# A decoder layer on one core: twelve small loads between weight chunks, three groups of transposes moved, and a projection that takes its chunks in pairs

## The chip, the core and the metric

The kernel runs on one core of a Trainium2 chip. A core has a matrix engine (TensorE, PE in the profile; its weight loads have a row of their own, PEld), three engines for elementwise work (VectorE = DVE, ScalarE = ACT, GpSimd = POOL) and SyncE (SP), which here only issues transfers. Each engine works through its own list of instructions in order and waits on semaphores for the others. Transfers between main memory (HBM) and the on-chip memory (SBUF) are issued by SP or POOL and carried out by 16 DMA engines. [...]

The metric is the device time of one execution in microseconds (us). The kernel before took 1500.24 us (median of three runs: 1500.24, 1496.19, 1501.05).

## The reference

One layer of a decoder with 256 positions and a width of 2048, in float32. What matters here:

```python
def reference(x, ...):                       # x: (1, 256, 2048)
    h = rms_norm(x, norm_mix_pre)
    y = hybrid_mixer(h, w_in, ...)           # two attention branches, gated, summed, @ w_out
    x = x + rms_norm(y, norm_mix_post)       # the second use of x; the scale norm_mix_post
    h = rms_norm(x, norm_ffn_pre)
    y = conv_ffn(h, w_up, conv_w, conv_b, w_down)
    return x + rms_norm(y, norm_ffn_post)

def hybrid_mixer(h, ...):
    c_q, c_kv, k_r, q_s, k_s, v_s, gates = split(h @ w_in)
    q  = rms_norm(c_q, g_q) @ w_q_up         # latent attention: c_q (512 wide), c_kv (256 wide)
    kv = rms_norm(c_kv, g_kv) @ w_kv_up
    ...                                      # o_a: dense causal, o_b: sliding window
    g = sigmoid(gates)
    merged = g[0] * (o_a @ w_o_mla) + g[1] * (o_b @ w_o_swa)
    return merged @ w_out

def conv_ffn(h, w_up, ...):                  # w_up: 2048 x 11264 (two halves of 5632)
    a, b = split(h @ w_up)
    c = conv_b + conv_w[0]*a[t-2] + conv_w[1]*a[t-1] + conv_w[2]*a[t]
    return (gelu(c) * b) @ w_down
```

## The kernel before, in words

**Products in three parts.** A float32 operand is split into a coarse part (`hi`) and the remainder (`lo`), both in a format that TensorE takes at full rate. A product is hi*hi + hi*lo + lo*hi, the sum of three matmuls.

**Weights come as chunks.** Every weight is read once from HBM. `wchunk` (L106) fetches 128 x 1024 numbers (512 KB) into one of three `raw` buffers by a transfer that SP issues; ACT casts it to `whi` (L124), DVE subtracts to `wlo` (L125). There are five `whi` and five `wlo` buffers, so the two engines can be some five chunks ahead of TensorE. A `raw` buffer is free for the next transfer when both casts of its chunk are done, a `whi` or `wlo` buffer when TensorE's last matmul on it is done.

**Two forms of product.** `gemm` (L153) holds the activations as TensorE's weights and streams 512 columns of the weight matrix: twelve matmuls of 512 columns per chunk (L149 to L151), into two accumulators of 128 rows each. `gemm_t` (L181), used for the up projection `w_up` alone, holds the weight matrix as TensorE's weights and streams the activations. The hi and lo parts of the 256 positions lie side by side, so that the hi part of a weight block meets both in one matmul of 512 columns (L189) and the lo part meets the hi half alone in a matmul of 256 columns (L193). One chunk is eight matmuls of 512 columns and then eight of 256, over four accumulators. The up projection has eleven blocks of 512 columns for each half (a and b); the first block of half a goes through `gemm`, which leaves 21 calls of `gemm_t` of eight chunks each, 168 chunks.

**Deferred work.** `at(t, f)` puts f on a list under step t, and `tick()`, called once per chunk after the chunk's matmuls, runs what stands under the current step. So a group of transposes that is put at `now[0] + 1` gets its place on TensorE behind the second chunk of the product that follows. The Tile scheduler may still move an instruction in an engine's list, except where `keep_in_program_order` or a manual schedule forbids it; the lists it made are shown below.

**The places that the change touches.**

- The latents c_q and c_kv: `latent` (L487) scales them and gives `tr` (L501), which transposes a pair of 128-column blocks on TensorE into one PSUM tile (`cqT`, `ckT`), each half followed by a cast on ACT and a subtraction on DVE (L224, L225). `k_rope` (L536) does the same for the rope key.
- The merge of the branches, once for each block of 512 columns: `gemm` with `wo_a` (w_o_mla, 8 chunks), then two DVE instructions per half of the rows (L772, L773) form `lta` = gate * product + the other branch, and `m_cols` (L749) transposes `lta` on TensorE in two groups of four (`mT`, L754), which become the operand of the product with `w_out`.
- `x2` and `gpost`: the second copy of x (eight tiles of 256 KB) and the scale of the norm after the mixer, spread to all 128 partitions (1 MB). POOL issues them (L744, L779) before and beside the first `wo_a` product. `gpost` is first read when the first `w_out` block is done (L791), `x2` when the last one is (`resid`, L800).
- The up projection: behind each half a, ACT and DVE run the convolution and the gelu (`conv_next`, L891, with `conv_a`), four pieces of 256 columns, under the steps of half b's first chunks; behind half b, `conv_b` (L896).

Of the kernel before, what the change touches and what calls it, by code (L numbers as in the profile page):

```python
# [19 lines left out]
P = 128  # L20
D = 2048
S = 256
NT = 2
# [18 lines left out]
def trunk_layer(ctx, tc, x, g_mix_pre, g_mix_post, g_ffn_pre, g_ffn_post, w_in, g_q, w_q, g_kv, w_kv,  # L42
                sinks, rel, wo_a, wo_b, w_out, w_up, conv_w, conv_b, w_down, rope_tab, strip_sel, out):
    nc = tc.nc
# [14 lines left out]
    def sb(pl, shape, name, dt=F32, tag=None, bufs=None):  # L59
        return pl.tile(shape, dt, name=name, tag=tag or name, **({"bufs": bufs} if bufs else {}))  # L60
# [45 lines left out]
    def wchunk(src, shape, own=None, rawp=None):  # L106
        i = cnt[0]
        cnt[0] += 1
        n = int(np.prod(shape))
        raw = rawp.tile([P, 1024], F32, name=f"raw{i}", tag="xraw") if rawp else \  # L110
            ring.tile([P, 1024], F32, name=f"raw{i}", tag="raw", bufs=RAW)
        dst = raw[:, :n]
        if len(shape) == 2:
            dst = dst.rearrange("p (a b) -> p a b", a=shape[0])
        elif len(shape) == 3:
            dst = dst.rearrange("p (a b c) -> p a b c", a=shape[0], b=shape[1])
        if len(shape) == 3:
            for k in range(shape[0]):
                nc.sync.dma_start(dst[:, k], src[:, k])
        else:  # L120
            nc.sync.dma_start(dst, src)
        hi, lo = ((own or ring).tile([P, 1024], F32R, name=f"w{part}{i}", tag="w" + part)
                  for part in ("hi", "lo"))
        act.copy(hi[:, :n], raw[:, :n])  # L124
        vec.tensor_tensor(lo[:, :n], raw[:, :n], hi[:, :n].bitcast(F32), op=ALU.subtract)  # L125
        return hi, lo
# [5 lines left out]
    def at(t, *fs):  # L132
        steps[max(t, now[0])].extend(fs)

    def tick():
        for f in steps.pop(now[0], ()):
            f()
        now[0] += 1

    def drain():  # L140
        while steps:
            tick()
# [37 lines left out]

    def gemm_t(xs, w, nk, c0, acc):  # L181

        for k in range(0, nk, 2):
            src = w[k * P:(k + 2) * P, c0:c0 + 512].rearrange("(a p) n -> p a n", p=P)
            hi, lo = wchunk(src, [2, 512])
            for j in range(2):
                for i in range(4):
                    c = j * 512 + i * P
                    pe.matmul(acc[i], hi[:, c:c + P], xs(k + j), start=k + j == 0, stop=False)  # L189
            for j in range(2):  # L190
                for i in range(4):
                    c = j * 512 + i * P
                    pe.matmul(acc[i][:, 0:256], lo[:, c:c + P], xs(k + j)[:, 0:256], start=False, stop=k + j == nk - 1)  # L193
            tick()

    def rsqrt(v, n, name, pl):
        y = sb(pl, [P, n], f"{name}_y")
# [323 lines left out]
    acc, _ = gemm(XH, XL, w_in, 0, KT, 0, 512)  # L521
    nrm, tr = latent(acc, QR, 32, cqh, cql, "cq")
    nrm()
    at(now[0] + 3, lambda tr=tr: tr(0))
    at(now[0] + 4, lambda tr=tr: tr(1))
    acc, _ = gemm(XH, XL, w_in, 0, KT, C_KV, KVR + ROPE)
    krd = []
    for t in range(NT):
# [12 lines left out]

    nrm, tr = latent(acc, KVR, 36, [ckh], [ckl], "ck")
    nrm()
    at(now[0] + 2, k_rope)
    at(now[0] + 3, lambda tr=tr: tr(0))


    ta_d = dram.tile([4, NT, P, 512], F32, name="ta_d")
# [190 lines left out]
    MH_, ML_ = pair_view(mth), pair_view(mtl)  # L739
    sb(p3, [P, 16], "pad_c")  # L740
    x2 = [[sb(p3, [P, 512], f"x2_{t}_{j}") for j in range(4)] for t in range(NT)]
    for t in range(NT):
        for j in range(4):
            pool.dma_start(x2[t][j], x[t * P:(t + 1) * P, j * 512:(j + 1) * 512])  # L744
    es6, p6 = open_pool("p6")
    esx, px = open_pool("px", bufs=EXTRA)
    es4, p4 = open_pool("p4")
# [1 line left out]
    def m_cols(p, ld):  # L749
        pt = pst.tile([P, 512], F32, name=f"mT{p}", tag="t")  # L750
        for i in range(2):
            for t in range(NT):
                c = (2 * (p % 2) + i) * P
                pe.transpose(pt[:, i * 256 + t * P:i * 256 + (t + 1) * P], ld[t][0][:, c:c + P], ident)  # L754
        split_to(mth[p][:, :], mtl[p][:, :], pt, 0.5)

    def merge_loads(j):
# [6 lines left out]
            ld.append((a, b))  # L764
        return ld

    for j in range(4):
        ld = merge_loads(j)
        acc, _ = gemm(AH, AL, wo_a, 0, KT, 512 * j, 512)
        for t in range(NT):  # L770
            a, b = ld[t]
            vec.scalar_tensor_tensor(a, a, 1.0, acc[t], op0=ALU.add, op1=ALU.mult)  # L772
            vec.tensor_tensor(a, a, b, op=ALU.add)  # L773
        for p in range(2):
            at(now[0] + 1 + p, lambda p=2 * j + p, ld=ld: m_cols(p, ld))


    gpost = sb(p6, [P, D], "gpost", tag="gp")
    pool.dma_start(gpost, g_mix_post.partition_broadcast(P))  # L779
    yg = [[sb(p6, [P, 512], f"yg_{t}_{j}", tag="f" + "ab"[t], bufs=4) for j in range(4)] for t in range(NT)]  # L780
    blocks = [(0, 512), (512, 512), (1024, 512), (1536, 256), (1792, 256)]
    NB = len(blocks)
# [56 lines left out]
    for b in range(4):  # L839
        c0, n = W_BLOCKS[b]  # L840
        last = b == 3
        acc, todo = gemm(MH_, ML_, w_out, 0, KT, c0, n, split=last, extra={i: (px,) for i in range(EXTRA)} if last else None)
        if b == 0:
            drain()
            es4.close()
            es8, p8 = open_pool("p8")
        if last:
            y_evac(acc, b, 0)
            resid(0)
            for f in todo:  # L850
                f()
            y_evac(acc, b, 1)
        else:
            for t in range(NT):
                y_evac(acc, b, t)
# [193 lines left out]
```

## Time and profile before

| what | value |
|---|---|
| median of three runs | 1500.24 us (1496.19 to 1501.05) |
| the profiled execution's own time | 1497.73 us |
| its span in the trace | 1495.9 us |
| granted TensorE clock, mean | 0.997 of full speed |
| TensorE busy | 1477.5 us (99%), 7853 matmuls |
| DVE, ACT busy | 988.6 us (66%), 802.2 us (54%) |
| moved by DMA | 285.52 MB, 191 GB/s on the mean |
| w_out, w_o_mla, w_up chunks, issue to landing (median) | 4.1, 4.5, 4.5 us |

How to read it: the page gives busy time for each engine and the chain of work that ended last. "L124" is a line of the kernel, and a group is named by what it writes and reads (`mT<-ident,lta`). A matmul's duration in a row (some 390 ns for 512 columns) holds its way through the array and overlaps the next one, so the rate is read from the distance of two starts. "[2.31 <-DVE lta L773]" behind a row means that the engine sat idle for 2.31 us before it, ended by that instruction. Times in rows are from the start of the span.

### The profile page before, as it was taken

How to read it: one execution, taken by the hardware profiler on the slowest of the kernel's cores; microseconds unless marked ns; L12 is line 12 of the kernel's file. 1: busy time of each engine (PE TensorE's matmuls, PEld its weight loads, DVE VectorE, ACT ScalarE, POOL GpSimd, SP SyncE). 2: the span in 40 equal slices, each digit the busy share in tenths (PEclk: the TensorE clock that was granted, in tenths of full speed). 3: DMA queues.
4: the chain of work that ended last, by engine and by line, in shares of the span. 5: the costliest groups of instructions: out<-in, count | busy, mean ns of one | idle time of the engine just before them, and what ended most of it. 6: DMA issues, size and time to landing. Idle time of an engine off the chain costs nothing.

```text
span 1495.9 us, 21394 instructions
## 1 busy us (share of the span) xinstructions
PE 1477.5 (99%) x7853; PEld 1265.2 (85%) x7853; DVE 988.6 (66%) x1775; ACT 802.2 (54%) x1332; POOL 66.8 (4%) x114
## 2 busy tenths in 40 slices
PE   8999999999999999999999999999999999999997
PEld 6888888888899987888888888888888888888887
DVE  5688884444766764565677877876444677787555
ACT  6588874434555553444575555564444555565442
POOL 2123210000000002000000000000000000000000
PEclk9999999999999999999999999999999999999999
DMA  7766656666655558766656556566556556655663
GB/s 235 223 177 166 167 169 191 208 210 208 180 158 160 167 160 288 250 208 197 207 170 193 184 178 185 179 193 209 196 190 197 174 176 211 195 184 182 200 197 113
DMA packets 160808, 285.52 MB, mean 191 GB/s; under 512 B 18419, under 2 KB 33893, under 8 KB 160448
## 3 DMA queue, kind: packets, MB, share of 16 engines
q1 hardware_dynamic: 154736, 264.81, 56.2%
q0 software_dynamic: 5968, 19.36, 5.2%
q8 instruction: 61, 1.00, 0.3%
q14 instruction: 43, 0.35, 0.1%
HBM read 277.79 MB, written 6.34 MB: 190 GB/s over the span
## 4 chain that ended last, share of the span: by engine, by line
PE 92%; DVE 3%; DMA 2%; ACT 2%; issue 1%; SPq 0%; DVEq 0%; ACTq 0%
PE accg L150 17%; PE accg L151 17%; PE accg L149 17%; PE accb L189 11%; PE acca L189 10%; PE accb L193 6%; PE acca L193 5%; DMA raw<-in_w_in_dram 1%; DVE wlo L125 1%; DMA raw<-in_w_o_mla_dram 1%; PE mpo L701 1%; PE ms L667 1%; ACT p L427 1%; ACT whi L124 1%; PE qn L630 1%
## 5 line engine op out<-in xcount | busy, mean ns | idle before, releaser
L125 DVE TENSOR_TENSOR wlo<-raw,whi 128x1024 fp32r<-128x1024 f32 (+2 forms) x501 | 608.7, 1216 | 439.0 <-ACT whi L124 436.4
L124 ACT CAST whi<-raw 128x1024 fp32r<-128x1024 f32 (+2 forms) x501 | 522.9, 1045 | 547.9 <-PE accg L151 297.4
L149 PE MATMUL accg<-whi,ah 128*128 128x512 f32 (+2 forms) x896 | 343.8, 384 | 0.4 <-ACT whi L124 0.4
L150 PE MATMUL accg<-wlo,ah 128*128 128x512 f32 (+2 forms) x896 | 341.3, 381 | 0.5 <-DVE wlo L125 0.5
L151 PE MATMUL accg<-whi,al 128*128 128x512 f32 (+2 forms) x896 | 340.8, 380 | 0.0
L151 PEld LDWEIGHTS accg<-whi,al 128*128 128x128 f32 x896 | 168.5, 188 | 31.4
L150 PEld LDWEIGHTS accg<-wlo,ah 128*128 128x128 f32 x896 | 168.6, 188 | 30.8 <-DVE wlo L125 1.6
L149 PEld LDWEIGHTS accg<-whi,ah 128*128 128x128 f32 x896 | 168.5, 188 | 29.9 <-ACT whi L124 1.1
L149 PE MATMUL accg<-whi,bh 128*128 128x512 f32 x272 | 107.3, 394 | 0.0
L150 PE MATMUL accg<-wlo,bh 128*128 128x512 f32 x272 | 106.4, 391 | 0.0
L151 PE MATMUL accg<-whi,bl 128*128 128x512 f32 x272 | 106.3, 391 | 0.0
L189 PE MATMUL accb<-bh,whi 128*128 128x512 f32 x352 | 88.6, 393 | 0.0
L189 PE MATMUL accb<-bl,whi 128*128 128x512 f32 x352 | 88.4, 393 | 0.0
L189 PE MATMUL acca<-bh,whi 128*128 128x512 f32 x320 | 80.3, 392 | 0.0
L189 PE MATMUL acca<-bl,whi 128*128 128x512 f32 x320 | 80.1, 392 | 0.0
L189 PEld LDWEIGHTS accb<-bh,whi 128*128 128x128 f32 x352 | 63.2, 189 | 11.6 <-ACT rfrow L836 0.3
L189 PEld LDWEIGHTS accb<-bl,whi 128*128 128x128 f32 x352 | 63.3, 189 | 11.3
L189 PEld LDWEIGHTS acca<-bh,whi 128*128 128x128 f32 x320 | 57.5, 189 | 10.6 <-DVE ds L953 0.3
L189 PEld LDWEIGHTS acca<-bl,whi 128*128 128x128 f32 x320 | 57.6, 189 | 10.3
L151 PEld LDWEIGHTS accg<-whi,bl 128*128 128x128 f32 x272 | 51.3, 189 | 10.8
L149 PEld LDWEIGHTS accg<-whi,bh 128*128 128x128 f32 x272 | 51.4, 189 | 10.4
L150 PEld LDWEIGHTS accg<-wlo,bh 128*128 128x128 f32 x272 | 51.4, 189 | 10.3
(339 smaller groups left out, 1934.3 us busy)
## 6 DMA issues: line engine op xcount, KB each, us to landing
raw<-in_ffn_w_up_dram SPq DMA_DIRECT2D x176, 512.0 KB, 4.5
raw<-in_w_in_dram SPq DMA_DIRECT2D x111, 512.0 KB, 4.3
raw<-in_ffn_w_down_dram SPq DMA_DIRECT2D x88, 512.0 KB, 4.4
raw<-in_w_o_swa_dram SPq DMA_DIRECT2D x32, 512.0 KB, 4.2
raw<-in_w_o_mla_dram SPq DMA_DIRECT2D x32, 512.0 KB, 4.5
raw<-in_w_out_dram SPq DMA_DIRECT2D x32, 512.0 KB, 4.1
raw<-in_mla_w_q_up_dram SPq DMA_DIRECT2D x48, 128.0 KB, 2.7
bias<-strip POOLq DMA_DIRECT2D x16, 256.0 KB, 4.0
```

The costliest lines, as they stand in the source:

```text
L124: act.copy(hi[:, :n], raw[:, :n])
L125: vec.tensor_tensor(lo[:, :n], raw[:, :n], hi[:, :n].bitcast(F32), op=ALU.subtract)
L149: pe.matmul(o, ah, bh, start=start, stop=False)
L150: pe.matmul(o, ah, bl, start=False, stop=False)
L151: pe.matmul(o, al, bh, start=False, stop=stop)
L189: pe.matmul(acc[i], hi[:, c:c + P], xs(k + j), start=k + j == 0, stop=False)
L193: pe.matmul(acc[i][:, 0:256], lo[:, c:c + P], xs(k + j)[:, 0:256], start=False, stop=k + j == nk - 1)
L427: act.activation(pb[:, i, a:b], pb[:, i, a:b], AF.Exp, bias=st["nm"][:, i, t:t + 1], accum_out=st["sm"][:, i, t:t + 1])
L630: pe.matmul(o, wh, ch(k), start=k == 0, stop=False)
L667: pe.matmul(o, w, v_, start=n == 0, stop=False)
L701: pe.matmul(o, w(t), p_[:, c], start=n == 0, stop=n == 5)
```

## The change

Three edits that do not depend on each other:

1. **Loads.** The eight transfers of `x2` leave POOL and go to SP, one at a time, under the steps 34, 37, ... 55 counted from the start of the `wo_a` product; `gpost` goes from one transfer of 1 MB to four of 256 KB, under the steps 19, 22, 25, 28. `keep_in_program_order` holds them at their places between SP's weight transfers. The `drain()` behind the first `w_out` block is taken out, since it would run the later steps at once.
2. **Transposes.** The groups of c_q go one step later (4 and 5 for 3 and 4), those of the rope key and of c_kv two steps (4 and 5 for 2 and 3), those of the merged rows one step (2 and 3 for 1 and 2).
3. **Pairs.** `gemm_t` fetches two chunks, runs the sixteen matmuls of 512 columns of both, and then the sixteen of 256. The steps tick behind each half of the 512s.

```diff
     def gemm_t(xs, w, nk, c0, acc):
-        for k in range(0, nk, 2):
-            src = w[k * P:(k + 2) * P, c0:c0 + 512].rearrange("(a p) n -> p a n", p=P)
-            hi, lo = wchunk(src, [2, 512])
-            for j in range(2):
-                for i in range(4):
-                    c = j * 512 + i * P
-                    pe.matmul(acc[i], hi[:, c:c + P], xs(k + j), start=k + j == 0, stop=False)
-            for j in range(2):
-                for i in range(4):
-                    c = j * 512 + i * P
-                    pe.matmul(acc[i][:, 0:256], lo[:, c:c + P], xs(k + j)[:, 0:256], start=False, stop=k + j == nk - 1)
-            tick()
+        for k in range(0, nk, 4):
+            ws = []
+            for kk in (k, k + 2):
+                ws.append(wchunk(w[kk * P:(kk + 2) * P, c0:c0 + 512].rearrange("(a p) n -> p a n", p=P), [2, 512]))
+            for n, (hi, _) in enumerate(ws):
+                for j in range(2):
+                    for i in range(4):
+                        c = j * 512 + i * P
+                        pe.matmul(acc[i], hi[:, c:c + P], xs(k + 2 * n + j), start=k + 2 * n + j == 0, stop=False)
+                tick()
+            for n, (_, lo) in enumerate(ws):
+                for j in range(2):
+                    for i in range(4):
+                        c = j * 512 + i * P
+                        pe.matmul(acc[i][:, 0:256], lo[:, c:c + P], xs(k + 2 * n + j)[:, 0:256], start=False,
+                                  stop=k + 2 * n + j == nk - 1)
...
-    at(now[0] + 3, lambda tr=tr: tr(0))
-    at(now[0] + 4, lambda tr=tr: tr(1))
+    at(now[0] + 4, lambda tr=tr: tr(0))
+    at(now[0] + 5, lambda tr=tr: tr(1))
...
-    at(now[0] + 2, k_rope)
-    at(now[0] + 3, lambda tr=tr: tr(0))
+    at(now[0] + 4, k_rope)
+    at(now[0] + 5, lambda tr=tr: tr(0))
...
-    for t in range(NT):
-        for j in range(4):
-            pool.dma_start(x2[t][j], x[t * P:(t + 1) * P, j * 512:(j + 1) * 512])
...
+    gpost = sb(p6, [P, D], "gpost", tag="gp")
+
+    def load_gpost(j):
+        c = slice(j * 512, (j + 1) * 512)
+        tc.keep_in_program_order(nc.sync.dma_start(gpost[:, c], g_mix_post[c].partition_broadcast(P)))
+
+    def load_x2(t, j):
+        tc.keep_in_program_order(nc.sync.dma_start(x2[t][j], x[t * P:(t + 1) * P, j * 512:(j + 1) * 512]))
+
+    for j in range(4):
+        at(now[0] + 19 + 3 * j, lambda j=j: load_gpost(j))
+        for t in range(NT):
+            at(now[0] + 34 + 12 * t + 3 * j, lambda t=t, j=j: load_x2(t, j))
...
-            at(now[0] + 1 + p, lambda p=2 * j + p, ld=ld: m_cols(p, ld))
-
-    gpost = sb(p6, [P, D], "gpost", tag="gp")
-    pool.dma_start(gpost, g_mix_post.partition_broadcast(P))
+            at(now[0] + 2 + p, lambda p=2 * j + p, ld=ld: m_cols(p, ld))
...
         if b == 0:
-            drain()
             es4.close()
             es8, p8 = open_pool("p8")
```

What the scheduler makes of it is seen in the engines' lists. In the names below, a number behind `raw`, `whi` and `wlo` is that of the chunk. Chunks 173 to 204 are those of `wo_a`, eight to a block, and 205 to 236 those of `w_out`; `accg_181` is the accumulator of the second `wo_a` block, `lta0` are the merged rows of the first.

TensorE in the second `wo_a` block, before: the first group of transposes `mT0` stands behind chunk 182.

```order
L150 MATMUL accg_181_1_6113<-wlo182_6135,bh1_4077 128x512
L151 MATMUL accg_181_1_6113<-whi182_6134,bl1_4085 128x512
L754 MATMUL mT0_6150<-ident_72,lta0_0_5946 128x128
L754 MATMUL mT0_6150<-ident_72,lta0_1_5950 128x128
L754 MATMUL mT0_6150<-ident_72,lta0_0_5946 128x128
L754 MATMUL mT0_6150<-ident_72,lta0_1_5950 128x128
L149 MATMUL accg_181_0_6112<-whi183_6159,bh2_4078 128x512
```

And now: it stands behind chunk 183, and the twelve matmuls of that chunk ahead of it.

```order
L150 MATMUL accg_181_1_6106<-wlo183_6146,bh2_4078 128x512
L151 MATMUL accg_181_1_6106<-whi183_6145,bl2_4086 128x512
L755 MATMUL mT0_6161<-ident_72,lta0_0_5939 128x128
L755 MATMUL mT0_6161<-ident_72,lta0_1_5943 128x128
L755 MATMUL mT0_6161<-ident_72,lta0_0_5939 128x128
L755 MATMUL mT0_6161<-ident_72,lta0_1_5943 128x128
L149 MATMUL accg_181_0_6105<-whi184_6170,bh3_4079 128x512
```

SP, in the stretch of the last `wo_a` and first `w_out` chunks, now: before, only the `raw` rows stood here, in the same order.

```order
L772 DMA gpost_5938<-in_norm_mix_post_dram 128x512
L121 DMA raw202_6559<-in_w_o_mla_dram 128x2x512
L121 DMA raw203_6577<-in_w_o_mla_dram 128x2x512
L121 DMA raw204_6595<-in_w_o_mla_dram 128x2x512
L121 DMA raw205_6647<-in_w_out_dram 128x2x512
L121 DMA raw206_6665<-in_w_out_dram 128x2x512
L121 DMA raw207_6683<-in_w_out_dram 128x2x512
L775 DMA x2_0_0_5921<-in_x_dram 128x512
L121 DMA raw208_6709<-in_w_out_dram 128x2x512
```

So each small transfer stands behind three weight transfers, and the fourth waits its turn behind it.

DVE in the up projection, where half a of block 2 (`acca2`) has just ended, before: the chunks 277 to 284 are half b's. The subtractions for 280 and 281 stand ahead of the convolution, which begins with `ca8`.

```order
L125 TENSOR_TENSOR wlo279_8629<-raw279_8626,whi279_8628 128x1024
L125 TENSOR_TENSOR wlo280_8666<-raw280_8663,whi280_8665 128x1024
L125 TENSOR_TENSOR wlo281_8703<-raw281_8700,whi281_8702 128x1024
L888 TENSOR_TENSOR ca8_8574<-ca8_8574,acca2_0_8344 128x256
L888 TENSOR_TENSOR ca9_8611<-ca9_8611,acca2_1_8345 128x256
L893 TENSOR_TENSOR ca8_8574<-ca8_8574,rfrow_7619 128x256
```

And now, the end of the same convolution: `wlo281` has gone from its head to a place behind 26 of its 32 instructions, and `wlo282` from behind 22 of them to behind 30.

```order
L889 TENSOR_TENSOR gg2_0_8345<-gg2_0_8345,rfrow_7622 128x256
L886 TENSOR_TENSOR uu10_8654<-uu10_8654,cc10_8653 128x256
L883 SCALAR_TENSOR_TENSOR cc11_8676<-ca11_8672,cvT_132,cc11_8676 128x254
L125 TENSOR_TENSOR wlo281_8706<-raw281_8703,whi281_8705 128x1024
L888 SCALAR_TENSOR_TENSOR gg2_1_8346<-uu10_8654,cc10_8653 128x256
L885 TENSOR_SCALAR uu11_8677<-uu11_8677 128x256
L889 TENSOR_TENSOR gg2_1_8346<-gg2_1_8346,rfrow_7622 128x256
L886 TENSOR_TENSOR uu11_8677<-uu11_8677,cc11_8676 128x256
L125 TENSOR_TENSOR wlo282_8712<-raw282_8709,whi282_8711 128x1024
```

The same stands in the other nine blocks whose half a goes through `gemm_t`. TensorE's list there has, per pair of chunks, sixteen rows of 512 columns and then sixteen of 256, where it had eight and eight twice.

## The prediction

> **What bounds the kernel now.** The page first: who is busy, and what the chain of work that ended last consists of.
>
> ```profile
> span 1495.9 us, 21394 instructions
> PE 1477.5 (99%) x7853; PEld 1265.2 (85%) x7853; DVE 988.6 (66%) x1775; ACT 802.2 (54%) x1332; POOL 66.8 (4%) x114
> PE 92%; DVE 3%; DMA 2%; ACT 2%; issue 1%; SPq 0%; DVEq 0%; ACTq 0%
> ```
>
> TensorE is the bound. No matmul is removed, so time can only come from where TensorE stands still, runs at a lower clock, or starts its matmuls farther apart than it could. The view of TensorE's waits has three that the edits touch (waited for; us in total, times, longest):
>
> ```profile
> PE mT L754 <- DVE lta L773: 2.3, 1, 2.3
> PE ckT L505 <- DVE ckl L225: 1.3, 1, 1.3
> PE cqT L505 <- DVE ptl L222: 0.2, 1, 0.2
> ```
>
> The 2.3 us lie in the second `wo_a` block. Busy times there by stretch (the last three columns: granted clock, share of the DMA engines, GB/s):
>
> ```profile
> 580.00:590.00 10.00, 10.00 (x46) 8.27 (x45) 1.48 (x2) 2.08 (x2) 0.00 (x0) 1.00 1.01 386
> 594.00:596.30 2.30, 0.23 (x2) 0.00 (x0) 2.30 (x4) 1.62 (x2) 0.00 (x0) 1.00 0.26 74
> 596.30:599.70 3.40, 3.09 (x9) 2.44 (x10) 3.17 (x5) 1.28 (x2) 1.08 (x2) 0.50 0.87 283
> ```
>
> From 580 to 590 the DMA engines are full; from 594 to 596.3 TensorE is idle; for the next 3.4 us it has half its clock. TensorE, DVE, POOL and ACT in time order:
>
> ```profile
> 593.84 0.39 PE L151 MATMUL accg<-whi,bl 128*128 128x512 f32 x1
> 596.54 1.41 PE L754 MATMUL mT<-ident,lta 128*128 128x128 f32 x4 [2.31 <-DVE lta L773]
> 597.61 0.77 PE L149 MATMUL accg<-whi,bh 128*128 128x512 f32 x1
> 598.18 0.63 PE L150 MATMUL accg<-wlo,bh 128*128 128x512 f32 x1
> ```
> ```profile
> 593.37 1.23 DVE L125 TENSOR_TENSOR wlo<-raw,whi 128x1024 fp32r<-128x1024 f32 x1 [2.10 <-ACT whi L124]
> 594.52 1.28 DVE L772 SCALAR_TENSOR_TENSOR lta<-lta,accg 128x512 f32<-128x512 f32 x2
> 595.71 1.29 DVE L773 TENSOR_TENSOR lta<-lta,lyb 128x512 f32<-128x512 f32 x2
> ```
> ```profile
> 573.53 4.25 POOL L744 DMA_DIRECT2D x<-in_x_dram  x8 [4.94 <-DMA ta_d<-ta]
> 578.93 0.53 POOL L779 DMA_DIRECT2D gpost<-in_norm_mix_post_dram  x1 [1.16 <-DMA x<-in_x_dram]
> ```
> ```profile
> 584.89 1.05 ACT L124 CAST whi<-raw 128x1024 fp32r<-128x1024 f32 x1 [5.89 <-DMA raw<-in_w_o_mla_dram]
> 588.97 1.05 ACT L124 CAST whi<-raw 128x1024 fp32r<-128x1024 f32 x1 [3.03 <-DMA raw<-in_w_o_mla_dram]
> ```
>
> Read backwards: the transposes wait for the merge (`lta`), which stands on DVE behind a subtraction, which waits for a cast, which waits 5.89 and 3.03 us for weight chunks. These are late because 3 MB of `x2` and `gpost`, issued from 573.5 to 579, share the DMA engines with them.
>
> **Term 1, the merge.** TensorE's last start before the gap is 593.84, the next 596.54: 2.70 us where a matmul of 512 columns takes 0.23 (below), so 2.5 are lost. Half the clock for 3.4 us loses another 1.7. Together 4.2 us. [...]
>
> Two edits cover this, either by itself. Without the 3 MB the chunks come on time; the first block's product ends two chunks before the gap (each 12 x 0.227 = 2.72 us), at 593.84 + 0.23 - 5.44 = 588.6, and the four merge instructions take 594.52 to 597.00, 2.5 us, so with a subtraction of 1.2 ahead they are done by 592.3. The transposes, one chunk later, come at 594.07 + 2.72 = 596.8: 4.5 us to spare. With the 3 MB still in the way the wait would be 0.2 us (597.00 less 596.8). What is then late is nothing near: the transposed rows are read by the product with `w_out`, and the last two groups, now behind its third and fourth chunk, by its seventh and eighth. I take the whole 4.2; bounds 2.5 (the clock falls anyway) and 4.4.
>
> **Term 2, the latents.**
>
> ```profile
> 219.82 0.38 PE L505 MATMUL ckT<-ident,ck 128*128 128x128 f32 x2
> 224.24 0.44 PE L505 MATMUL ckT<-ident,ck 128*128 128x128 f32 x2 [1.28 <-DVE ckl L225]
> ```
> ```profile
> 221.47 1.05 ACT L124 CAST whi<-raw 128x1024 fp32r<-128x1024 f32 x1 [0.68 <-DMA raw<-in_w_in_dram]
> 222.43 0.46 ACT L224 ACTIVATE ckh<-ckT,gmat 128x256 fp32r<-128x256 f32 x1
> ...
> 227.49 1.05 ACT L124 CAST whi<-raw 128x1024 fp32r<-128x1024 f32 x1 [2.31 <-PE accg L151]
> ```
> ```profile
> 223.70 0.48 DVE L225 SCALAR_TENSOR_TENSOR ckl<-ckT,gmat,ckh 128x256 fp32r<-128x256 f32 x1
> ```
>
> The second pair writes the PSUM tile that the first pair's cast and subtraction still read. These stand behind a chunk's cast and subtraction on ACT and DVE, and at 221.47 that cast was still waiting for its weights; at 227.49 the casts wait for TensorE instead, so the supply has caught up. Two chunks later the pair meets a supply that is nearly there, but the order stays: a cast of 1.05 begins when TensorE ends a chunk, `ckh` 0.46, the subtraction 1.23, `ckl` 0.48, together 3.2 us against the 2.72 + 0.3 until the second pair. That leaves 0.2 to 0.5 of the 1.28. With 0.1 of cqT's 0.2 I take 1.0 us. Bounds: -0.5 (c_q's groups now stand together beside the last attention unit and may wait instead) and 1.5. Nothing else waits for these tiles soon.
>
> **Term 3, the pairs.** Starts of long rows of one width, and of the up projection's chunks in the chain of waits:
>
> ```profile
> 239.71 0.39 PE L150 MATMUL accg<-wlo,ah 128*128 128x512 f32 x1
> ...
> 255.81 0.39 PE L149 MATMUL accg<-whi,bh 128*128 128x512 f32 x1
> ```
> ```profile
> 1472.77 0.28 PE L149 MATMUL accg<-whi,ah 128*128 128x256 f32 x1
> ...
> 1486.44 0.28 PE L149 MATMUL accg<-whi,gh 128*128 128x256 f32 x1
> ```
> ```profile
> 843.59 1.84 PE acca L189 x8
> ...
> 865.93 1.84 PE accb L189 x8
> ...
> 1019.57 1.84 PE accb L189 x8
> ```
>
> The first has 71 steps of 512 columns, 16.10 / 71 = 0.2268 us; the second 114 steps of 256, 13.67 / 114 = 0.1199; the third 63 chunks, 175.98 / 63 = 2.793. Eight and eight would be 1.814 + 0.959 = 2.773, so each change of width and back costs 0.020 us. There are 168; the pairs leave 84: 84 x 0.020 = 1.7 us. The row of 114 steps shows that long runs of 256 keep their rate, so I price the switch and not its length. Bounds 0 and 2.0.
>
> **Costed at nothing.** The supply in the up projection. `wlo` of one chunk in each of ten blocks now stands behind 26 instructions of the convolution.
>
> ```profile
> 867.24 0.74 DVE L888 TENSOR_TENSOR ca<-ca,acca 128x256 f32<-128x256 f32 x2
> ...
> 874.74 1.22 DVE L125 TENSOR_TENSOR wlo<-raw,whi 128x1024 fp32r<-128x1024 f32 x1
> ```
> ```profile
> raw<-in_ffn_w_up_dram SPq DMA_DIRECT2D x176, 512.0 KB, 4.5
> ```
>
> Before, 22 instructions took 867.24 to 874.74, 0.34 each; 26 take 8.9. Begun at 866.3, when DVE is free, they end at 875.2, and the subtraction at 876.4. TensorE begins this half at 865.93; its third pair follows at 877.1 (a pair is 2 x 2.773) and needs this `wlo` after sixteen matmuls of 512, at 880.7: 4.3 us to spare. The `raw` buffer is freed late too: SP waits with the next chunk until 876.4, it lands 4.5 later, is cast by 882.0, and TensorE needs it as second of the fourth pair at 865.93 + 16.6 + 1.8 = 884.4: 2.4 us to spare, the thinnest place of the change. Queued behind that transfer are only later chunks, each with more.
>
> The twelve loads on SP: 256 KB at the 386 GB/s of the full stretch are 0.68 us each, and the transfer behind them is later by that. What covers it:
>
> ```profile
> ACT whi L124 <- PE accg L151: 50.8, 34, 1.7
> ```
>
> From 600 to 755 the casts wait for TensorE 34 times, 50.8 us: they are ahead. If that cover were gone it would be 12 x 0.68 = 8.2 us.
>
> **Sum.** 4.2 + 1.0 + 1.7 = 6.9 us. The profiled execution took 1497.73 us, its span 1495.9: 1490.8 and 1489.0 after. The three runs shown lie 1.4 us above the profiled one on the mean (1499.16), so I predict 1492 for the median.
>
> **Rivals.**
>
> *The up projection starves (slower).* If burst and reload together come 2.4 us later than worked out, TensorE waits in each of ten blocks. For: ACT and DVE hand the convolution to each other, and the casts there already wait for transfers. Against: the same burst was followed by no wait of TensorE before. At 4 us later it costs 10 x 1.6 = 16 us: 1508. It makes the change slower from 3.6 us on.
>
> *The small loads delay the weights.* They stand in the queue of the weights now and not beside it. For: the 580 to 590 stretch shows what 3 MB can do. Against: the cover above, and that one comes per three chunks. Fully exposed, 1492 + 8.2 = 1500. [...]
>
> *The waits only move.* The groups, one or two chunks later, meet a supply as late as before, so terms 1 and 2 give nothing: 1499.2 - 1.7 = 1497.5. Against: the 5.89 us wait is for transfers that shared the engines with loads now gone.
>
> *A switch costs by the length of the run before it.* Then term 3 is 0: 1494. Against: the long row above, though no row shows 16 and 16.
>
> **How the numbers follow.** Forecast 0.70 (its own range 1489 to 1495.5), starvation 0.09, delayed weights 0.07, moved waits 0.08, length 0.06. This kernel's runs tell 0.3% (4.5 us) from no change; the bound for faster is 1495.7. Of the forecast's chance 0.05 may fall inside it with the scatter of the runs. Faster 0.65 + 0.06 = 0.71, same 0.05 + 0.07 + 0.08 = 0.20, slower 0.09. The range, 1487 to 1500, takes in the bounds of the three terms and the two cases in between, and leaves out starvation.
>
> **What would show it.** Term 1: no wait of `mT` on `lta`, clock 1.00 throughout 580 to 600, casts there waiting for TensorE. Term 2: a wait of `ckT` under 0.5 us. Term 3: pairs 5.57 us apart where two chunks took 5.59. Starvation: TensorE's waits name `whi` or `wlo` in the up projection, ten times; then the forecast is wrong. Delayed weights: casts in the `w_out` product waiting for `raw` and TensorE for casts.

## The result and the profile after

The changed kernel took 1522.03 us (median of five runs, 1518.93 to 1522.19) against 1497.62 for the kernel before (five runs): a ratio of 1.015, 95% interval 1.0132 to 1.0168. By the medians it is slower by 24.4 us, outside the range on record. What happened is the first rival, the starving up projection, which had 9% and stood at 1508. One execution of a later run, that of the loads alone, took 6038.36 us, four times as long as any other; it is left out of its median below, and nothing rests on it.

The page of the changed kernel, its span, TensorE's busy time and its chain by engine:

```profile
span 1520.4 us, 21379 instructions
PE 1487.0 (98%) x7853; PEld 1270.5 (84%) x7853; DVE 988.0 (65%) x1775; ACT 803.6 (53%) x1332; POOL 62.7 (4%) x105
PE 71%; DVE 12%; DMA 11%; ACT 5%; issue 1%; ACTq 0%; DVEq 0%; SPq 0%
```

TensorE had 92% of the chain before and has 71% now; DVE, the DMA engines and ACT took the rest. Its waits (us in total, times, longest) say where:

```profile
PE accb L197 <- DVE wlo L125: 15.4, 12, 3.1
PE accg L150 <- DVE wlo L125: 3.6, 2, 2.0
PE ckT L509 <- DVE ckl L229: 0.7, 1, 0.7
```

`accb L197` are the 256-column matmuls of half b, the half under which the convolution runs. The 3.6 us are in the product with `w_down`, whose first chunks queue behind the late ones. The wait of `mT` is gone. One such place in TensorE's own time, and the granted clock from the last 0.7 us of the gap on (third number from the end):

```profile
915.07 2.08 PE L197 MATMUL accb<-bh,wlo 128*128 128x256 f32 x16
916.98 3.81 PE L191 MATMUL accb<-bl,whi 128*128 128x512 f32 x16
923.94 2.08 PE L197 MATMUL accb<-bl,wlo 128*128 128x256 f32 x8 [3.15 <-DVE wlo L125]
```
```profile
923.20:930.00 6.80, 5.79 (x21) 5.11 (x22) 6.06 (x10) 1.52 (x3) 0.00 (x0) 0.50 0.56 165
```

By stages, from TensorE's starts in the four traces (us; the last two are experiments below):

| stage | before | after | edits 1 and 2 alone | after, fourth raw buffer |
|---|---|---|---|---|
| first `x2T` (start of the norm behind `w_out`) | 744.5 | 740.2 | 740.1 | 740.3 |
| up projection, half b of block 0 and blocks 1 to 5 | 246.9 | 257.0 | 246.9 | 246.0 |
| first product with `w_down` between | 130.7 | 134.7 | 130.7 | 130.7 |
| up projection, blocks 6 to 10 | 223.5 | 236.2 | 223.5 | 222.7 |
| span | 1495.9 | 1520.4 | 1491.7 | 1490.4 |

Ahead of the up projection the change wins 4.4 us; in it and in the two products with `w_down` it loses 28.7 (10.1, 4.0, 12.7 and 1.9). The waits above are 19.0 of that; three stretches at half clock in it, 13.7 us together, cost up to 6.8 more.

### The profile page after: what moved, and what is told of

Read it like the earlier page. It is cut to its first block, busy times and chain, and to the rows that moved or that the text cites. A ratio compares the mean times of both kernels' runs of the same rounds, so it can differ in the third digit from the quotient of the medians.

```text
span 1520.4 us, 21379 instructions
## 1 busy us (share of the span) xinstructions
PE 1487.0 (98%) x7853; PEld 1270.5 (84%) x7853; DVE 988.0 (65%) x1775; ACT 803.6 (53%) x1332; POOL 62.7 (4%) x105
## 4 chain that ended last, share of the span: by engine, by line
PE 71%; DVE 12%; DMA 11%; ACT 5%; issue 1%; ACTq 0%; DVEq 0%; SPq 0%
PE accg L150 17%; PE accg L151 16%; PE accg L149 16%; DMA raw<-in_ffn_w_up_dram 9%; PE acca L191 5%; DVE wlo L125 5%; PE accb L191 3%; ACT whi L124 3%; PE acca L197 2%; PE accb L197 2%; DMA raw<-in_ffn_w_down_dram 1%; DMA raw<-in_w_in_dram 1%; DVE cc L882 1%; DVE cc L883 1%; PE mpo L705 1%
## 5 line engine op out<-in xcount | busy, mean ns | idle before, releaser
L191 PE MATMUL accb<-bh,whi 128*128 128x512 f32 x352 | 84.5, 392 | 0.0
L191 PE MATMUL acca<-bl,whi 128*128 128x512 f32 x320 | 76.6, 391 | 0.0
L191 PE MATMUL acca<-bh,whi 128*128 128x512 f32 x320 | 76.5, 391 | 0.0
L191 PEld LDWEIGHTS accb<-bh,whi 128*128 128x128 f32 x352 | 64.5, 188 | 12.7 <-ACT rfrow L848 0.3
L191 PEld LDWEIGHTS acca<-bl,whi 128*128 128x128 f32 x320 | 58.7, 188 | 11.8 <-ACT whi L124 0.5
L197 PE MATMUL accb<-bl,wlo 128*128 128x256 f32 x352 | 50.7, 296 | 15.4 <-DVE wlo L125 15.4
L197 PEld LDWEIGHTS accb<-bl,wlo 128*128 128x128 f32 x352 | 47.4, 200 | 20.6 <-DVE wlo L125 19.2
```

Of the source, the lines that this page charges most:

```text
L191: pe.matmul(acc[i], hi[:, c:c + P], xs(k + 2 * n + j), start=k + 2 * n + j == 0, stop=False)
L197: pe.matmul(acc[i][:, 0:256], lo[:, c:c + P], xs(k + 2 * n + j)[:, 0:256], start=False, stop=k + 2 * n + j == nk - 1)
```

## The experiments

Three theories stood at the start. **A:** DVE's list now puts one subtraction of each block behind the convolution; its `raw` buffer stays taken, SP's transfers pause, and the lead over TensorE runs out. **B:** the twelve loads on SP delay the weights. **C:** the pairs hold too many of the five `whi` and `wlo` buffers.

**Edit 3 alone, and edits 1 and 2 alone.** The kernel before with the new `gemm_t`; and the changed kernel with the old one:

```diff
-        for k in range(0, nk, 2):
+        for k in range(0, nk, 4):
...
```

> Edit 3 alone on the kernel before; loads and transposes as they were. Theory A (burst): in the pairs two wlo buffers come free at the end of a half together, so one subtraction that stood ahead of the convolution on DVE falls behind it, its raw buffer stays full, SP cannot load, and the up projection and the two down products lose what they lost in the changed kernel: 24.5 + 4.4 = 29 us over the span, about 1526. Theory B (loads): the twelve loads on SP, or the order that came with them, starve the up projection; the pairs alone then gain 1.7 us, about 1496. Theory C (buffers): five wlo buffers are too few for pairs, in whatever order: 1526 too.

> Edits 1 and 2 without the pairs. Theories A and C: no wait on wlo in the up projection, 4.4 us less than before, about 1493. Theory B: the waits stay, about 1520.

Edit 3 alone: ratio 1.0206 (1.0186 to 1.0225), median 1528.66 us. Edits 1 and 2 alone: 0.9976 (0.9967 to 0.9986), 1493.68 us. Of edit 3 alone:

```profile
PE accb L197 <- DVE wlo L125: 16.9, 13, 3.9
PE accg L150 <- DVE wlo L125: 2.1, 3, 1.5
```

The pairs starve TensorE whether the loads were moved or not. B falls.

**A fourth raw buffer, and the convolution spread.** Both keep all three edits. The first takes every fourth chunk of `gemm_t` into one more `raw` buffer; the five `whi` and `wlo` stay:

```diff
+    def fourth():
+        rx[1] += 1
+        return rx[0] if rx[1] % 4 == 0 else None
...
-                ws.append(wchunk(w[kk * P:(kk + 2) * P, c0:c0 + 512].rearrange("(a p) n -> p a n", p=P), [2, 512]))
+                ws.append(wchunk(w[kk * P:(kk + 2) * P, c0:c0 + 512].rearrange("(a p) n -> p a n", p=P), [2, 512], rawp=fourth()))
...
+            rx[0] = p7
```

The second puts the four pieces of the convolution under every second step:

```diff
-                at(now[0] + i, lambda i=i: conv_next(acc[i], 4 * c + i, gs))
+                at(now[0] + 2 * i, lambda i=i: conv_next(acc[i], 4 * c + i, gs))
```

> The changed kernel with a fourth raw buffer, used by every fourth chunk of the up projection only; the lists of DVE and ACT stay as in the changed kernel, the subtraction still stands behind 26 instructions of the convolution. Theory A: SP can load one more chunk during the convolution and refills four at a time, so the lead comes back before the next block: no wait on wlo, 1497.6 - 4.4 - 1.7 = about 1491.5. Theory C: wlo buffers are as few as before, so the waits stay, about 1520.

> The changed kernel with the four pieces of the convolution one per pair of chunks (steps 0, 2, 4, 6) where they came one per chunk (0 to 3); three raw buffers, five wlo buffers. On DVE the first held subtraction now stands behind 4 instructions of the convolution, the second behind 10, the third behind 20. Theory A: raw buffers come free from the start, no or little waiting, 1491 to 1496. Theory C: about 1520.

Fourth buffer: 0.9965 (0.9952 to 0.9977), 1492.2 us. Spread: 0.9968 (0.9956 to 0.9981), 1492.66 us. Neither has a wait of `accb` or `acca` left. C falls, since the number of `whi` and `wlo` did not change; what was short was the way from memory to them. The wait of SP's queue for subtractions between 775 and 1020 us (total, times, longest) shows the pause that A names. Before, after, and spread:

```profile
SPq L121 <- DVE wlo L125: 168.3, 68, 8.3
```
```profile
SPq L121 <- DVE wlo L125: 195.4, 75, 11.5
```
```profile
SPq L121 <- DVE wlo L125: 175.0, 74, 4.7
```

**Edit 1 alone, edit 2 alone.** The two that remain, each on the kernel before. Edit 2 is taken with all three of its places, of which the last is shown:

```diff
...
-            at(now[0] + 1 + p, lambda p=2 * j + p, ld=ld: m_cols(p, ld))
+            at(now[0] + 2 + p, lambda p=2 * j + p, ld=ld: m_cols(p, ld))
```

> The kernel before with edit 1 alone (the twelve loads on SP between weight chunks, the emptying of the step list gone); transposes and chunks as before. Theory L (edit 1 lets the weight chunks of w_o_mla arrive on time, and the merge wait goes with it): no wait of mT on lta, clock 1.00 between 594 and 600 us, the first x2T about 4.2 us earlier than the 744.51 of before, time 3.5 to 4.5 us less, about that of both edits together (ratio 0.9976); the ckT wait stays at about 1.3 us. Rival T (it is the later place of the transposes that removes the wait): the mT wait stays near 2.3 us with the half clock behind it, first x2T within 1 us of 744.5, ratio 1.000. Rival D (the loads delay weights on SP): new waits of accg for whi or wlo between 600 and 745 us, up to 8 us.

> The kernel before with edit 2 alone (c_q, c_kv, rope key and merged rows transposed one or two steps later); loads on POOL and chunks one by one as before. My prediction said that either of the two edits covers the merge by itself, here with a wait of 0.2 us left. Theory E (either is enough): mT waits at most 0.3 us, clock 1.00, first x2T at 739.9 to 741, time 4 to 5 us less. Theory L (only edit 1 removes the cause, the late chunks): the transposes still meet a late merge, and the wait only moves to a matmul that needs a late chunk: waits of mT or accg between 580 and 605 us of 1.5 us or more in sum, ratio above 0.9985. By both, ckT waits 0.4 to 1.0 us.

The loads alone: 0.999 (0.9982 to 0.9999), 1495.88 us (median of eleven). The transposes alone: 0.9976 (0.9966 to 0.9986), 1493.6 us, as much as both together. In neither profiled execution is there a wait of `mT` or a lower clock between 580 and 600 us. With the transposes alone the merge ends nearly as late as before, and they arrive just behind it. DVE, then TensorE:

```profile
595.16 1.29 DVE L773 TENSOR_TENSOR lta<-lta,lyb 128x512 f32<-128x512 f32 x2
596.36 1.22 DVE L125 TENSOR_TENSOR wlo<-raw,whi 128x1024 fp32r<-128x1024 f32 x1
```
```profile
596.35 0.39 PE L151 MATMUL accg<-whi,bl 128*128 128x512 f32 x1
596.58 0.60 PE L754 MATMUL mT<-ident,lta 128*128 128x128 f32 x4
```

The merge ends at 595.16 + 1.29 = 596.45, and the transposes start at 596.58. The wait of `ckT` is 1.7 us with the loads alone and 0.8 with the transposes alone, 0.9 of the 1.5 us between their spans (1493.0 and 1491.5). These executions of the loads alone reach from 1493.69 to 1498.3, and the four above 1496.5 that show a mean clock of 0.997 suggest that there the gap still opens at times; no trace of such a one was taken.

**The fourth buffer without the pairs.** Edits 1 and 2, the old `gemm_t`, and the fourth buffer:

```diff
-            hi, lo = wchunk(src, [2, 512])
+            hi, lo = wchunk(src, [2, 512], rawp=fourth())
```

> Edits 1 and 2 without the pairs, and a fourth raw buffer in gemm_t as in the run before. Tells what the fourth buffer does where nothing starves, and prices the pairs cleanly: the difference to the changed kernel with the fourth buffer is the pairs and nothing else. Theory A (the fourth buffer only keeps up the lead): time as without it (1493.7, within 0.7 us), up projection halves 246.9 and 223.5 us from first to last, and the pairs are worth 84 x 0.020 = 1.7 us beside it. Rival G (the fourth buffer is a gain of its own, which hid the starving rather than curing it): 1492 or less, up projection shorter by 0.5 us or more per half, and the pairs are worth under 1 us.

0.9982 (0.9973 to 0.9991), 1493.92 us, span 1491.6: the buffer is worth nothing where nothing starves (A). With it the two halves of the up projection take 246.9 + 223.5 us one by one and 246.0 + 222.7 in pairs. Unrounded that is 1.6 us, 0.019 for each of the 84 switches saved.

**Four buffers for whi and wlo, no pairs.** The kernel before with `RING` set to four. DVE's list then shows the move that the pairs made, one more subtraction behind the convolution:

```diff
-RING = 5
+RING = 4
```

> The kernel before, chunks one by one, but with four whi and four wlo buffers in place of five. Then the list of DVE has the same move that the pairs caused: in each block one subtraction more stands behind the convolution's 22 instructions. Theory A (the subtraction behind the burst holds its raw buffer, SP's transfers stop for it, and the refill is too slow to win the lead back before the next burst): TensorE waits for whi or wlo in the up projection, ten blocks, 10 to 35 us in sum, though no chunk is paired. Rival P (it is the pairs that hold their buffers too long, and the place of one subtraction does not matter): with four buffers the lead is 2.8 us shorter, 8.1 in place of 10.9, and the burst takes 3.5 of it as before: no wait, time within 2 us of the kernel before.

1.0082 (1.0069 to 1.0095), 1508.87 us, but not for the reason that A gave. The up projection's halves take 246.8 and 223.5 us, as before, with no wait in them. Of the 10.9 us by which the span is longer, 8.4 are lost ahead of the up projection, most of them in one stall ahead of the norm behind `w_out`, with half the clock (0.50) for 10.2 us from 750.4 on, still within it, and 2.3 behind the last matmul. The stall:

```profile
PE x2T L810 <- issue: 7.1, 1, 7.1
```

So the place of one subtraction does not starve the projection. A, as it was put, falls too. What the kernels differ in was then counted chunk by chunk: SP's two long pauses per block of 16 chunks (under the convolution, and under `conv_b`), and the lead, from the end of a chunk's cast to TensorE's first matmul on it (both worked out from the traces by the order of the lists, us). The chunks are those of blocks 1 to 5; the lead "ahead of" a convolution is that of the last chunk cast before it:

| kernel | first block's pauses | later blocks | lead ahead of the first convolution, and of the first chunk fetched after it | lead ahead of the second one, and after |
|---|---|---|---|---|
| before | 8.7, 4.3 | 8.5 to 8.7, 4.2 to 4.4 | 10.9, 7.4 | 10.9, 7.4 |
| before, `RING` four | 8.7, 4.5 | 8.5 to 8.7, 4.2 to 4.5 | 8.1, 4.6 | 8.0, 4.4 |
| after | 10.0, 6.0 | 11.4 to 11.9, 5.6 to 6.7 | 11.5, 3.4 | 8.1, 0.6 |
| after, fourth raw | 10.0, 4.7 | 10.0, 4.6 to 4.8 | 11.8, 6.6 | 11.8, 6.8 |

This gives theory **F**. In the pairs' lists 26 instructions of the convolution stand ahead of the subtraction and not 22, and 11 of `conv_b` and not 9, so both pauses are longer and the lead is not back when the next convolution begins; and that one then begins late. (With the fourth buffer DVE's list changed too: 9 instructions of `conv_b` stand there and not 11, and so they do in the run with the convolution spread. That alone is not the cure: with `conv_b` spread, below, 4 stand there, and TensorE still starves.) ACT's list has a cast ahead of the copies `ca` with which the convolution starts. In the first block of the changed kernel TensorE begins half b at 816.58, and the copies are there in time; in the second it begins at 861.11:

```profile
815.15 1.05 ACT L124 CAST whi<-raw 128x1024 fp32r<-128x1024 f32 x1 [1.00 <-DMA raw<-in_ffn_w_up_dram]
816.41 1.20 ACT L898 COPY ca<-acca 128x256 f32<-128x256 f32 x4 [0.22 <-PE acca L197]
...
863.12 1.05 ACT L124 CAST whi<-raw 128x1024 fp32r<-128x1024 f32 x1 [1.33 <-PE accb L191]
864.08 1.18 ACT L898 COPY ca<-acca 128x256 f32<-128x256 f32 x4
```

The cast at 863.12 is of a chunk whose transfer was issued at 858.46, and such a transfer takes 4.6 us in this stretch: it is the transfer that it waited for, though the row names TensorE. The copies come 3.0 us behind the half's end and not 0.2 before it. With the fourth buffer TensorE begins this half at 861.33 and the copies come at 861.17:

```profile
859.62 1.05 ACT L124 CAST whi<-raw 128x1024 fp32r<-128x1024 f32 x1 [0.72 <-PE acca L195]
861.17 1.20 ACT L904 COPY ca<-acca 128x256 f32<-128x256 f32 x4 [0.51 <-PE acca L201]
```

The work on DVE is then the same, 8.9 us from its first row to the subtraction; in the changed kernel it starts 3.4 us behind the half's end and not 0.4, and the subtraction behind it comes as much later, and SP's next transfer (two issues: start of the first, until the end of the second):

```profile
864.47 0.75 DVE L899 TENSOR_TENSOR ca<-ca,acca 128x256 f32<-128x256 f32 x2 [1.43 <-ACT ca L898]
...
873.35 1.22 DVE L125 TENSOR_TENSOR wlo<-raw,whi 128x1024 fp32r<-128x1024 f32 x1
```
```profile
863.07 11.93 SPq L121 DMA_DIRECT2D raw<-in_ffn_w_up_dram  x2
```

The same of the kernel before:

```profile
867.35 9.04 SPq L121 DMA_DIRECT2D raw<-in_ffn_w_up_dram  x2
```

So F says that late transfers make the convolution late, and that a late convolution stops the transfers for longer.

**Pairs in every other block, and the second half spread.** Two tests of F. The first sends even blocks through the old `gemm_t` (`gemm_1`); the second spreads `conv_b` alone:

```diff
...
-            gemm_t(HS, w_up, KT, 512 * c, acc)
+            (gemm_t if c % 2 else gemm_1)(HS, w_up, KT, 512 * c, acc)
...
```
```diff
-            at(now[0] + i, lambda i=i: conv_b(acb[i], 4 * c + i, gg[i], slot0 + i))
+            at(now[0] + 2 * i, lambda i=i: conv_b(acb[i], 4 * c + i, gg[i], slot0 + i))
```

> The changed kernel, with the pairs kept only in every other block of the up projection (odd ones, 1, 3, 5, 7, 9); the even blocks take their chunks one by one as before. In the paired blocks DVE's list is that of the change (26 convolution instructions ahead of a subtraction, 11 in the second half). Theory F (one paired block only draws down the lead, from 11 us to 8; the harm comes when the next convolution begins with a lead that is not back, because the cast on ACT that still waits for its transfer stands ahead of the convolution's copies and makes the burst late too): each paired block now begins with a full lead, TensorE's waits for whi or wlo in the up projection are under 1 us in sum, and half of the pairs' gain comes in, 42 x 0.020 = 0.8 us beside the 1493.7 of the version without pairs: 1492.9, ratio 0.997. Rival S (a paired block starves by itself, whatever came before; the first one was spared because the gemm blocks ahead of it left more on chip): five of ten blocks starve, half of the 28 us that the pairs cost: about 1507, ratio 1.007.

> The changed kernel with the second half's elementwise work (conv_b) put under every second step in place of every step; the convolution behind the first half stays as dense as in the change, with 26 instructions ahead of a subtraction. Theory F (the lead must be back before the next convolution; what keeps it from coming back is the hold of 11 instructions in the second half, where SP's transfers pause for 6.0 us, and then the late burst): without that hold the lead is back to 11 us at the next convolution, the burst begins under 1 us after the half ends in every block, waits for whi or wlo under 1 us in sum, time 1492 to 1493, ratio 0.997. Rival B (the dense convolution alone is too much for three raw buffers): waits of 5 us or more stay, time 1498 to 1520, and the burst still begins 2 us and more late from the second block on.

Every other block: 1.0042 (1.0028 to 1.0056), 1503.23 us. Second half spread: 1.0043 (1.0028 to 1.0059), 1503.96 us. Their waits, in this order:

```profile
PE accb L197 <- DVE wlo L125: 4.8, 5, 1.1
PE accg L150 <- DVE wlo L125: 2.5, 3, 2.0
PE accb L191 <- ACT whi L124: 0.9, 1, 0.9
```
```profile
PE accb L197 <- DVE wlo L125: 6.7, 8, 1.1
PE accb L191 <- ACT whi L124: 1.4, 3, 0.8
```

Both of F's forecasts were wrong: there is less starving, about a third to a half, but one block taken one by one does not bring the lead back (11.2 us ahead of the first convolution, 5.3 ahead of the second, 6.0 ahead of the third), and without the second pause it comes back to 9.3 and not to 11. What F lacked was the rate of the refill. Behind a long pause, where the three `raw` buffers limit SP, it issues a chunk every 2.11 to 2.32 us on the mean of the first six steps; with four buffers the first four steps take 1.60 us each. So, as an estimate from these steps, a block's supply takes two pauses and fourteen steps:

| kernel | pauses + 14 steps | TensorE's block |
|---|---|---|
| before | 8.67 + 4.34 + 14 x 2.17 = 43.4 | 16 x 2.793 = 44.7 |
| after, first block | 10.04 + 5.98 + 14 x 2.15 = 46.1 | 8 x 5.566 = 44.5 |
| second half spread | 10.04 + 3.5 + 14 x 2.2 = 44.3 | 44.5 |
| after, fourth raw | 10.04 + 4.69 + 14 x 1.60 = 37.1 | 44.5 |

With six-step means of 2.16 to 2.23 us the kernel before had about 1 us to spare per block (0.5 to 1.4), 1 to 3%. The changed one lacks 1.6 in its first paired block by the sum (its 16 transfers took 45.9 us there, from one long pause to the next), and once it is late its pauses grow (47.5 to 49.0 us per block in the next three). The spread one, whose longest steps under `conv_b` are 3.2 to 3.8 us, has nothing left to regain a lead with: its first block took 45.3 us, more than the sum. The last row is the most favourable, since it takes the four fastest steps for all; with 1.9 us, the highest of its six-step means, it is still 41.3.

**More loads, no pairs.** If it is a budget, anything that adds to it should starve the kernel without pairs too. Edits 1 and 2, the old `gemm_t`, and eight loads per block that nobody reads:

```diff
+            for q in range(8):
+                at(now[0] + 2 + 2 * q, lambda q=q: spare_load(c, q))
```

> Edits 1 and 2 without the pairs, and eight further loads of 256 KB on SP in each block of 16 chunks of the up projection, into a tile that nothing reads; no engine's list of elementwise work changes. Theory G (a budget: SP's 16 transfers of a block take two pauses of 8.67 and 4.3 to 4.8 us and fourteen steps of about 2.2 us, 43.8 us, against 44.7 us of TensorE; whatever adds more than about 1 us per block starves it, paired or not): eight loads at 0.68 us are 5.4 us where nothing overlaps, so that a block lasts up to 49 us; TensorE waits for whi or wlo from the second or third block on, 10 to 45 us in sum, time 1503 to 1540, and the convolution's first copies begin late after the half, as in the changed kernel. Rival P (it takes the pairs, which hold buffers longer; one by one, a lead of 11 us covers such loads): no waits of whi or wlo over 1 us in sum, time 1493.7 plus at most 2.

0.9979 (0.997 to 0.9988), 1495.05 us, 1.4 more than without the loads; span 1496.5.

```profile
PE accg L150 <- DVE wlo L125: 2.0, 2, 1.8
PE accb L193 <- DVE wlo L125: 0.9, 1, 0.9
```

By its median this is what rival P said. By its waits it is not quite: the profiled execution, which was the slowest of the ten (1498.25 us), has 2.9 us of them, where P allowed 1 and G forecast 10 to 45. The lead tells more: that of the last chunk fetched ahead of the long pause is 10.9, 9.8, 7.6 and 5.8 us in blocks 1 to 4, some 2 us less each time. In block 5 TensorE waits 0.9 us, and 1.8 more in the product behind it. SP's 16 transfers took 46.1, 46.8 and 47.0 us in blocks 2 to 4. So the drift of G is there, but against the 43.4 us of the table a load of 256 KB cost the supply an estimated 0.3 to 0.5 us ((46.1 - 43.4) / 8 to (47.0 - 43.4) / 8) and not 0.68. And SP's pauses hardly grow with the lead that low (9.8 us at most, 11.9 in the changed kernel), though the convolution's copies begin 3.9, 5.6 and 6.9 us behind the half's end in blocks 3 to 5. Without the pairs the lead drains, and a late start alone does not lengthen the pause by much; with the pairs' order a low lead and longer pauses come together. How the loss divides between longer lists and late starts was not separated further.

**All but edit 1.** Edits 2 and 3 with the fourth buffer; `x2` and `gpost` stay on POOL:

> Edits 2 and 3 with the fourth raw buffer, without edit 1 (x2 and gpost stay on POOL). Tells whether the twelve moved loads are worth anything beside the later transposes. Theory E (the transposes alone remove the merge wait, and the loads' share is nothing): time as with all three edits and the fourth buffer, 1492.2 within 0.7 us, no mT wait. Rival L (the moved loads carry a part): 1493.5 or more, with a wait of mT, or of accg for whi or wlo, between 590 and 745 us.

0.996 (0.9947 to 0.9972), 1491.82 us: the lowest of all, though its interval and that of the fourth buffer with all three edits (0.9952 to 0.9977) cover each other. Its page:

```profile
span 1490.0 us, 21367 instructions
PE 92%; DVE 3%; ACT 2%; DMA 2%; issue 1%; DVEq 0%; SPq 0%; ACTq 0%
```

The moved loads are worth nothing beside the moved transposes.

## Why the prediction was wrong

**The step that failed** is in "Costed at nothing": "Queued behind that transfer are only later chunks, each with more." The working of the first block was close. 4.3 us to spare were worked out for the held subtraction; 4.26 were found (chunk 265, the one that stands there in the first paired block). 2.4 were worked out for the chunk reloaded behind it; 3.4 were found. But the sentence takes for granted that the lead of 11 us is there again at the next convolution, and that was never added up. The rows to do it with were at hand: each pause, the steps of SP between, and TensorE's 44.7 us per block. With 26 instructions for 22 and 11 for 9 at 0.34 us, 1.4 + 0.7 us are added to a supply with about 1 to spare; measured in the first paired block, the pauses grew by 1.4 and 1.6. The second step that failed is the start of the burst, "when DVE is free": it starts when ACT has made its copies, and these stand behind a cast that may wait for its transfer.

**The rival** named the right engine, tile and place, and its size was off: 1.6 us in each of ten blocks were assumed, and the loss was 28.7 us, as lateness carries over from block to block and into the product with `w_down`. The condition put on it, "2.4 us later than worked out", was the wrong one: the first block was not late at all.

**Term 1**, the merge: right that either edit closes the gap in the trace. The wait left with the transposes alone was put at 0.2 us; it was none, with 0.13 to spare. Terms 1 and 2 were to bring 5.2 us; in the traces the up projection begins 4.4 us sooner. In medians edits 1 and 2 bring 1493.68 against 1496.62 (0.9976). The mean clock of the kernel before is 0.999 in some of its executions and 0.997 in others, as in the profiled one; this suggests that the stretch at half clock does not occur in each of them, and where it does not, there is less to win than the trace shows.

**Term 2**, the latents: the wait of `ckT` fell from 1.3 to 0.7 us, not to 0.2 or 0.5; the 1.0 us was about 0.4 too much.

**Term 3**, the pairs' own price: right. Where nothing is late, pairs are 5.56 to 5.57 us apart, against 5.586 for two chunks:

```profile
816.58 3.82 PE L191 MATMUL accb<-bh,whi 128*128 128x512 f32 x16
820.23 2.08 PE L197 MATMUL accb<-bh,wlo 128*128 128x256 f32 x16
822.14 3.82 PE L191 MATMUL accb<-bh,whi 128*128 128x512 f32 x16
```

1.7 us was put down, 1.6 was measured. With the supply restored, the kernel took 1492.2 us, and 1491.82 without edit 1, where 1492 was predicted. That this fits so closely is partly luck: the spans differ by 5.5 us (1495.9 to 1490.4) and the medians by 4.4 (1496.62 to 1492.2), not by 6.9, and the sum started from 1499.16, above the later medians of the kernel before. The starving that the sum left out was 30 us (1522.03 to 1492.2).

**Delayed weights** and **waits only move** did not occur: with edits 1 and 2 alone the only waits for `wlo` are 0.5 us in all, and none is for `lta` or `whi`. **Switch cost by length** did not either, as the 5.56 us show.

## What to carry to other kernels

A buffer that is ten microseconds ahead says nothing by itself: add up, for a whole period, what the supply takes (its pauses and its fastest steps) and set it against what the consumer takes; a change that lengthens a pause is safe only up to that difference. Reordering the consumer's matmuls changes when buffers are freed, and so the order that a scheduler gives to the other engines; compare those lists and price every instruction that now stands ahead of a producer. Where work of the consumer's results stands behind a producer's instruction on one engine, a late supply delays it, and may then be delayed by it.

## What the runs showed of the hardware

A gap of TensorE of 1.9 us was followed by at least 3.3 us at half the clock, one of 1.8 us was not. The first is in the run of edit 3 alone, where the wait of `ckT` (1.88 us) ended at 224.77; the second in the run with more loads, where one of 1.78 us ended at 1036.07 (columns as above, the granted clock third from the end):

```profile
225.70:229.00 3.30, 3.30 (x9) 2.54 (x9) 0.65 (x2) 0.02 (x1) 0.00 (x0) 0.50 0.88 268
```
```profile
1036.10:1039.50 3.40, 3.40 (x15) 2.83 (x16) 2.53 (x3) 0.17 (x1) 0.00 (x0) 1.00 0.56 189
```

The stretches at half clock between the matmuls were 3.41 us long in the kernel before (from 596.29, in the last 0.25 us of the gap of 2.31) and 6.83, 3.41 and 3.41 us in the changed kernel (from 923.16, in the last 0.8 us of the gap of 3.15, from 1042.63 and from 1343.00). With `RING` four the clock was at half for the 10.2 us from 750.4 on; the gap of 7.14 ended at 754.95.

The length of a gap did not decide alone. In the run of edit 3 alone (mean clock 0.990) one of 1.72 us, until 927.43, was followed by half the clock from 928.71, and with alternating pairs (0.996) two of 1.05 and 1.13 us, until 921.50 and 923.85, by half the clock from 924.25; the five longest gaps of the kernel with the second half spread (0.998), 0.96 to 1.13 us and far apart, left the clock alone.

The changed kernel's trace has both cases. The stretch from 1042.63 came behind a gap of 2.04 us, until 1041.23, and the one from 1343.00 with two of 2.11 and 1.12 us, until 1340.71 and 1343.05. The clock stayed at 1.00 behind a gap of 1.56 us, until 1411.64, and behind each of three times two gaps: 1.30 and 1.13 us until 1018.93 and 1021.27, 1.31 and 1.13 until 1292.02 and 1294.36, 1.18 and 1.13 until 1389.60 and 1391.94. Behind the one of 2.04 and the one of 1.56:

```profile
1042.70:1046.00 3.30, 3.30 (x9) 2.53 (x8) 1.08 (x1) 0.88 (x1) 0.00 (x0) 0.50 0.83 289
```
```profile
1411.60:1420.00 8.40, 8.36 (x37) 6.89 (x38) 4.21 (x5) 2.25 (x3) 0.00 (x0) 1.00 0.67 214
```

What decides between such gaps was not shown.
